# Moving one tile's gate chain, the x^T scaling and one weight load to other slots in a hybrid decoder layer

## The chip, the cores and the metric

The kernel runs on one core of a Trainium2 chip. The metric is device time in microseconds (us). The time before is the median of three runs, 1319.21 us (1318.01 to 1319.58).

## What is computed

The reference is a decoder layer with two kinds of token mixers that share one input and one output projection (batch 1, 2048 positions, width 1024, float32):

```python
xn = rms_norm(h, ln_g)
proj = jnp.einsum('bsd,de->bse', xn, w_in)
b_gate, c_gate, x_conv, g_conv, x_lru, g_lru = jnp.split(proj, splits, axis=-1)
y_conv = short_conv_mixer(b_gate, c_gate, x_conv, conv_w)
y_conv = headwise_rms_norm(y_conv, N_CONV_HEADS, conv_out_g) * jax.nn.silu(g_conv)
y_lru = rg_lru_mixer(x_lru, lru_conv_w, lru_conv_b, w_a, b_a, w_i, b_i, lam)
y_lru = headwise_rms_norm(y_lru, N_LRU_HEADS, lru_out_g) * jax.nn.silu(g_lru)
h = h + jnp.einsum('bse,ed->bsd', jnp.concatenate([y_conv, y_lru], axis=-1), w_out)
...
# rg_lru_mixer, on u = causal_depthwise_conv(x_lru, width 4) + bias:
r, i = sigmoid(gate maps of u per head)
a = exp(8 * r * log_sigmoid(lam))
h_t = a_t * h_{t-1} + sqrt(1 - a_t^2) * (i_t * u_t)      # along the positions
```

The layer's final `rms_norm` follows. All sums are in float32.

## The kernel before

**Numbers.** Every float32 matrix operand is cut into a high part (a cast by ScalarE to fp32r) and a low part (value minus high part, by VectorE). One block product is three matmuls: high by high, high by low, low by high (`mm`, L1009). In names of tiles, `s` is a weight operand (high and low side by side), `th` and `tl` are the high and low parts of the x^T operand, `raw` a raw weight piece of 256 KB, `traw` a raw piece of x^T.

**Steps and slots.** The input projection is made in 24 steps for each half of the positions (1024 each), named "l" (recurrent tile: x_lru and its gate g_lru), "a" and "b" (convolution: c_gate and x_conv, then b_gate and g_conv). Each step makes four 128x512 result blocks called 11, 12, 21 and 22 and hands each to a `put` function. The first four steps of the first half (`plain`, `products`) use plain products, since the operand set isn't complete yet; from step 4 on a seven-product scheme is used, with operands `T[0..6, j]` of x^T (j = 0..3) and `Sn[n][0..6]` of the weights. Before each of these products `tick()` is called: that is one slot, with 12 matmuls. `at(k, f)` puts `f` off to the k-th slot from now. All instructions are given out in the order in which this Python program runs them; each engine, and SyncE's queue of transfers (SP), takes its own in that order. So a slot number is a place in every engine's queue, not a time.

**The first tile.** `lru0 = lru(0, 0)` (L696) is the recurrent step 0. Its blocks 11 and 21 are made from unnormalised x^T and multiplied by the row norms later (`RAW`, then `lru0(11, None, rsb[0])`). After block 12 has come, `put` lists the rest of the tile by slot: `c0`, `cj` (the width-4 convolution, u), `sth`/`stl` (the cut of u), `gates(0)`, `gates(1)` (small matmuls on TensorE, L740), `sigs` (sigmoids), `s0` to `s5` (products, tanh, exp, sqrt, and `s5` the scan over positions), `out_` (`finish`: gain and gate, store, square, sums by head). `u` is a tile with one buffer: the next recurrent tile's `c0` writes the buffer that this tile's `s5` and, before, its output use.

**The other work of that stage.** `squares` and `rs0` make the row norms, `roots` turns them into a row (`rsb[0]`), `second(j)` makes the second block of x^T, `scaled(j)` multiplies the raw x^T by the norms and casts it, `scaled_lo(j)` makes its low part, `bit(j)` makes the sums of x^T blocks that operands 1, 2 and 6 need. `s_hi`, `s_lo` cut raw weights for the plain steps. `after1`, `after2`, `after3` hand these out among the slots of the steps 1, 2 and 3: slots 1 to 4, 5 to 12 and 13 to 20. Slot 21 is the first of step 4.

**Step 4 and on.** In a step the first product goes to a bank that ScalarE copies away (`q1`, L1435) before the second product of the same bank may start; between the two lies a slot with the seventh product of the step before, which step 4 does not have.

**The second half.** Operands of the weights are read back from `sd` in device memory (`s<-sd`, `s_loads`, L238) except for three steps (`redone`: 27, 28 and 29), whose raw weights are loaded anew into four of eight `raw` pieces (`load_s`, L326) and cut again. At the half's start (steps 24 and 25) the same pieces hold raw x^T (`traw`) until `Change.sixth` (L472) has used them in the last slot of step 25. `load_next(n + 2)` in slot s = 3 of a step gives the load out.

Of the kernel before, what the change touches and what calls it, by code (L numbers as in the profile page):

```python
# [14 lines left out]
AF = mybir.ActivationFunctionType  # L15
ALU = mybir.AluOpType

P = 128
D = 1024
S = 2048  # L20
C = 512
NC = S // C
NB = C // P
# [15 lines left out]
def hymba_kernel(ctx: ExitStack, tc: tile.TileContext, x, xt, w_in, par, lamc, w_gate, w_out, final_g, out):  # L39
# [103 lines left out]
    def at(slots, *fs):  # L143
        if slots == 0:
            for f in fs:
                f()
        else:
            due.append([slots, fs])
# [12 lines left out]
    def tt(out, a, b, op, eng=None):  # L161
        (eng or nc.vector).tensor_tensor(out=out, in0=a, in1=b, op=op)  # L162
# [483 lines left out]
            summed[0] = 0  # L646
            at(0 if h else 7, lambda: head_norms(h))

    def finish(d0, h, kt, y, sil, gain, to=None):
        z = sil if to is None else to  # L650

        def f1():
            nc.vector.scalar_tensor_tensor(out=z, in0=y, scalar=gain, in1=sil,
                                           op0=ALU.mult, op1=ALU.mult)

        def store():
            for i in range(2):
                nc.sync.dma_start(yd[2 * h + i][:, :, kt, :].rearrange("b p t -> p b t"),
                                  z[:, i * C:(i + 1) * C].rearrange("p (b t) -> p b t", b=NB))

        at(d0, f1)
        at(d0 + (1 if kt == KT and h == 0 else 2), store)
        at(d0 + 2, lambda: nc.scalar.activation(out=y, in_=y, func=AF.Square))
        at(d0 + 3, lambda: head_sums(h, kt, y))

    def silu(g, late=0, eng=None):
        sg = [None]

        def f1():
            sg[0] = wt("ig", "sg", bufs=IG)  # L670
            nc.scalar.activation(out=sg[0], in_=g, func=AF.Sigmoid)  # L671

        at(2 + late, f1)
        at(4 + late, lambda: tt(g, g, sg[0], ALU.mult, eng or nc.gpsimd))

# [15 lines left out]
    LO, HI = slice(0, 64), slice(64, P)  # L693
    N2 = 2 * C

    def lru(h, k, late=0, early=0):  # L696
        o1 = wt("o1", "xl", n=N2 + 4)
        g = wt("o2", "gl", bufs=O2)
        if h == 0:
# [32 lines left out]
        def gates(i):  # L732
            sl = slice(i * C, (i + 1) * C)
            if i == 0:
                v["r"], v["i"] = wt("r", "r"), wt("ig", "i", bufs=IG)
            v["ps"] = ps = []
            for j in range(2):
                ps.append(pss.tile([P, C], F32, tag="s", name="gate"))
                for n in range(2):
                    nc.tensor.matmul(ps[j], v["gw"][n][:, j, :], v["st"][j][:, sl],  # L740
                                     start=(n == 0), stop=(n == 1))

        def sigs(i):
            sl = slice(i * C, (i + 1) * C)
            for j, (hi, lo) in enumerate(((LO, HI), (HI, LO))):
                for g_, src, bias in ((v["r"], hi, BA), (v["i"], lo, BI)):
                    nc.scalar.activation(out=g_[hi, sl], in_=v["ps"][j][src], func=AF.Sigmoid,  # L747
                                         bias=pt[src, bias + k:bias + k + 1])
# [28 lines left out]
                nc.vector.tensor_copy(hl[:, k:k + 1], r[:, N2 - 1:N2])  # L777

        def out_():
            finish(0, h, KT + k, v["r"], g, pt[:, LG + k:LG + k + 1], v["u"] if h == 0 and k == 0 else None)  # L780

        def gw():
            v["gw"] = load_gate_w(k)
# [1 line left out]
        def put(which, bank, other):  # L785
            dst = {11: o1[:, 4:4 + C], 12: o1[:, 4 + C:4 + N2], 21: g[:, 0:C], 22: g[:, C:N2]}[which]
            combine(dst, bank, other)
            if other is RAW:
                return
            if which == 12:  # L790
                at(1, c0)
                at(2, lambda: cj(1), lambda: cj(2), keep, gw)
                at(3, lambda: cj(3))
                for slots, *fs in ((5 - early, sth), (6 - early, stl), (8, lambda: gates(0)), (8, lambda: sigs(0)),
                                   (10, lambda: gates(1)), (11 - h - early, lambda: sigs(1)), (12, s1, s0),
                                   (13, s1b), (14, s2, s3), (15, s4), (16, s5), (17, out_)):
                    at(slots + late, *fs)
            if which == 21:
                silu(g, late, nc.vector if late or not h else None)

        return put

# [253 lines left out]
    with tc.manual_schedule(engines={ENG.PE, ENG.Activation, ENG.DVE, ENG.Pool, ENG.SP}):  # L1056
# [44 lines left out]
        def s_lo(m, i, eng=None):  # L1101
            low(Wr[m][i], Sp[m][i], eng)
# [54 lines left out]
                products(0, raw[0], part, j, (0, 4), j == 0)  # L1157
        for b in range(NB, 2 * NB):
            norm_rows(b)
        lru0 = lru(0, 0)  # L1160
        lru0(11, raw[0][0], RAW)
        lru0(21, raw[0][1], RAW)

# [2 lines left out]
        def squares(b, eng=None):  # L1166
            for n in range(2):
                v, acc = xh[b][n], (rs0, rest)[n][:, b:b + 1]
                if eng is None:
                    nc.scalar.activation(out=v, in_=v, func=AF.Square, accum_out=acc)  # L1170
                else:
                    eng.scalar_tensor_tensor(out=v, in0=v, scalar=1.0, in1=v, op0=ALU.mult, op1=ALU.mult,
                                             accum_out=acc)

        squares(0)
        squares(1)
        squares(2, nc.vector)

        def second(j):
            for n, tag in ((1, "tl6"), (3, "th6")):  # L1180
                tr[j][n] = tp_.tile([P, C], F32, tag=f"{tag}{j}", name="traw")
            for i in range(2):
                turn(1, j + i * NB, tr[j][2 * i + 1], i)
            B12 = T[3, j] = t_tile(3, j)
            nc.scalar.copy(B12[0], tr[j][1])
            Tp[j].hi(5)
            low(tr[j][1], B12)
            Tp[j].lo(5)
# [4 lines left out]
                    second(j - 2)  # L1193
                products(1, raw[1], part, j, (0, 4))

        squares(3)
        tt(rs0, rs0, rest, ALU.add)
        nc.scalar.activation(out=rs0, in_=rs0, func=AF.Sqrt, scale=1.0 / D, bias=eps)
        nc.vector.reciprocal(out=rs0, in_=rs0)
        conv0 = conv_a(0, 0)  # L1200
        conv0(21, raw[1][1], RAW)

# [7 lines left out]
        def scaled(j):  # L1210
            for i in (0, 4):
                v = tr[j][i // 2]
                nc.vector.scalar_tensor_tensor(out=v, in0=v, scalar=gain(j + i), in1=rsb[0],  # L1213
                                               op0=ALU.mult, op1=ALU.mult)
                Tp[j].hi(i)

        def scaled_lo(j):
            for i in (0, 4):
                Tp[j].lo(i)
# [3 lines left out]
            nc.sync.dma_start(sd[0][i], S0[i].bitcast(F32))  # L1223
        c12, c22 = bank(), bank()
        for j in range(NB):
            if j + 2 < NB:
                second(j + 2)
            for cc, n in ((c12, 0), (c22, 2)):
                mm(cc, Sp[0], T, n, j, j == 0, False, k=3)
                mm(cc, Sp[0], T, n + 1, j, False, j == NB - 1, k=5)  # L1230
                if j == 1 and n == 0:
                    roots()
                    lru0(11, None, rsb[0])
                    lru0(21, None, rsb[0])
            if j >= 1:
                scaled(j - 1)
        scaled(3)
        lru0(22, c22, None)
        lru0(12, c12, None)
        second_half()  # L1240
# [40 lines left out]
                yield which, cc[which]  # L1281

        def after1(s):
            if s < 2:
                for i in (2 - 2 * s, 3 - 2 * s):
                    s_hi(2, i)
                for i in (2 - 2 * s, 3 - 2 * s):
                    s_lo(2, i)
            if s % 2 == 0:
                scaled_lo(s // 2)  # L1290
            do_bits(2)
            if s == 2:
                conv0(11, raw[1][0], rsb[0])
                conv0(22, kept[22], None)
# [6 lines left out]
        Wr.append(load_s(3))  # L1301

        def after2(s):
            if s in (0, 4):
                scaled_lo(2 + s // 4)
            if s % 2 == 0:
                s_hi(3, (2, 3, 0, 1)[s // 2])
            do_bits(1)
            if s % 2 == 0:
                s_lo(3, (2, 3, 0, 1)[s // 2])  # L1310
            if s > 5:
                for j in (2 * s - 12, 2 * s - 11):
                    T[6, j] = t_tile(6, j)
                    nc.scalar.copy(T[6, j][0], t6[j])

        put = conv_b(0, 0)
        for which, b in plain(2, (22, 12, 11, 21), after2):
# [3 lines left out]
        def after3(s):  # L1321
            if s in (1, 2, 3, 4, 6, 7):
                prep(4, (0, 1, 2, 3, 0, 4, 5)[s - 1])
            if s >= 6:
                js = (2 * s - 12, 2 * s - 11)
                for j in js:
                    T[3, j] = t_tile(3, j)
                    nc.scalar.copy(T[3, j][0], tr[j][1])
                for j in js:
                    low(tr[j][1], T[3, j])  # L1330
                at(s - 5, lambda: [low(t6[j], T[6, j]) for j in js])

        put = lru(0, 1)
        for which, b in plain(3, (11, 12, 22, 21), after3):
            if which == 12:
                kept[0] = b
            else:
                put(which, b, None)
# [4 lines left out]
        for n in range(PLAIN, N):  # L1343
# [31 lines left out]
            for s in range(6 if late else 8 if new or last else 7):  # L1375
# [33 lines left out]
                elif s > 0:  # L1409
                    if i == 2 and not late and held[0] is None or i == 1 and late:  # L1410
                        held[0] = []
                    if i != 2 or kind != "o" or not late:
                        prep(n + 1, s - 1)
                if s == 3:
                    load_next(n + 2, 3 if late else 4)
                if i == 6 and not late and s < 4:
                    if pend is not None:
# [90 lines left out]
```

## Time and profile before

| | us |
|---|---|
| median of 3 runs (lowest, highest) | 1319.21 (1318.01, 1319.58) |
| profiled execution, its own time | 1316.47 |
| its span, first to last instruction | 1314.5 |
| TensorE (PE) busy | 1285.9 (98%) |
| VectorE (DVE) busy | 1034.5 (79%) |
| ScalarE (ACT) busy | 753.8 (57%) |
| GpSimd (POOL) busy | 157.0 (12%) |
| granted TensorE clock, mean over the span | 0.993 |

The profiled execution took 2.0 us more than its span, and 2.7 us (0.2%) less than the median. "PE" is a matmul, "PEld" a weight load, "SPq" a transfer being issued by SyncE. In the timeline a row has start, length, engine, line, operation, output and inputs, shape, count, and in brackets the idle time of the engine before it and what ended it. `L162` is the helper `tt` for every elementwise VectorE operation on two tiles, so tiles tell more than lines there.

### The profile page before, as it was taken

The page shows a single profiled execution, that of the slowest core. Times are in us where ns is not written, and L with a number is a line of the kernel's source. Part 1 is how long each engine was busy: PE and PEld are TensorE (multiplying, and loading weights), DVE is VectorE, ACT ScalarE, POOL GpSimd, SP SyncE. Part 2 cuts the span into 40 slices and gives each one's busy share as a digit, 9 for nine tenths or more (in the row PEclk, how much of TensorE's full clock was granted, in tenths as well). Part 3 has the DMA queues.
Part 4 walks back from the last instruction along what each step waited for, and adds up shares of the span by engine and source line. Part 5 has one row for each costly group of instructions (what it writes and reads, how often), then busy time and mean ns, then how long its engine had stood idle before and what let it go on. Part 6 is the DMA issues. An engine that isn't in the chain of part 4 may idle for free.

```text
span 1314.5 us, 16625 instructions
## 1 busy us (share of the span) xinstructions
PE 1285.9 (98%) x5666; PEld 1060.5 (81%) x5666; DVE 1034.5 (79%) x1343; ACT 753.8 (57%) x1152; POOL 157.0 (12%) x143
## 2 busy tenths in 40 slices
PE   9979999999999999899999999999999999999997
PEld 8758888888888888677888888888888888888886
DVE  6788897999999998968566676667549877659886
ACT  8676867676675767665554545364457433445443
POOL 0000000233323320001010110102011000000000
PEclk9989999999999999999999999999999999999999
DMA  9206887898999888521889999999779897698754
GB/s 349 73 16 229 296 306 259 297 349 285 339 308 327 297 295 296 168 89 45 261 305 296 335 354 331 343 342 376 239 268 325 269 272 249 214 403 298 243 178 160
DMA packets 158244, 351.08 MB, mean 267 GB/s; under 512 B 16976, under 2 KB 51792, under 8 KB 158160
## 3 DMA queue, kind: packets, MB, share of 16 engines
q1 hardware_dynamic: 153552, 333.97, 73.5%
q0 software_dynamic: 4320, 15.73, 3.1%
q8 instruction: 45, 0.74, 0.2%
q14 instruction: 39, 0.32, 0.1%
q10 hardware_dynamic: 288, 0.32, 0.1%
HBM read 216.59 MB, written 133.37 MB: 266 GB/s over the span
## 4 chain that ended last, share of the span: by engine, by line
PE 82%; DVE 9%; DMA 4%; ACT 2%; issue 2%; SPq 0%; POOL 0%; DVEq 0%; ACTq 0%; POOLq 0%
PE bank L1014 78%; PE gate L740 2%; DVE tl L162 2%; PE bank L1151 2%; DMA tl<-td 1%; DMA s<-so 1%; DVE s L162 1%; DVE traw L162 1%; DMA raw<-yd 1%; DVE ob L162 1%; DVE u L712 0%; PE spin L541 0%; DVE traw L1213 0%; DMA s<-sd 0%; DVE st L162 0%
## 5 line engine op out<-in xcount | busy, mean ns | idle before, releaser
L1014 PE MATMUL bank<-th,s 128*128 128x512 f32 x3568 | 1109.4, 390 | 9.0 <-DMA s<-sd 5.6
L1014 PEld LDWEIGHTS bank<-th,s 128*128 128x128 f32 x3568 | 671.3, 188 | 151.6 <-DMA s<-sd 6.1
L1014 PE MATMUL bank<-tl,s 128*128 128x512 f32 x1784 | 695.4, 390 | 1.7 <-DVE tl L162 1.7
L1014 PEld LDWEIGHTS bank<-tl,s 128*128 128x128 f32 x1784 | 335.7, 188 | 72.0 <-DVE tl L162 2.1
L162 DVE TENSOR_TENSOR s<-raw,s 128x512 fp32r<-128x512 f32 (+1 forms) x151 | 104.0, 710 | 25.0 <-ACT s L212 20.5
L212 ACT CAST s<-raw 128x512 fp32r<-128x512 f32 x140 | 84.7, 618 | 42.8 <-PE bank L1014 29.2
L162 POOL TENSOR_TENSOR s<-raw,s 128x512 fp32r<-128x512 f32 x39 | 72.7, 1875 | 198.4 <-ACT s L212 141.1
L162 DVE TENSOR_TENSOR tl<-traw,th 128x512 fp32r<-128x512 f32 x92 | 61.5, 709 | 21.1 <-ACT th L450 10.7
L162 DVE TENSOR_TENSOR s<-s,s 128x512 fp32r<-128x512 f32 x105 | 74.3, 708 | 0.0
L212 ACT CAST s<-s 128x512 fp32r<-128x512 f32 x105 | 65.0, 619 | 10.2 <-DVE s L162 10.1
L712 DVE SCALAR_TENSOR_TENSOR u<-xl,pt,u 128x1024 f32<-128x1024 f32 x48 | 61.8, 1288 | 7.9 <-ACT u L708 7.4
L1435 ACT COPY q<-bank 128x512 f32<-128x512 f32 x57 | 33.4, 585 | 49.7 <-PE bank L1014 47.1
L162 POOL TENSOR_TENSOR gb<-gb,sg 128x1024 f32<-128x1024 f32 x8 | 20.1, 2509 | 308.3 <-ACT sg L671 308.3
L831 DVE SCALAR_TENSOR_TENSOR t<-p,pt,t 128x1024 f32<-128x1024 f32 x32 | 44.7, 1396 | 13.2 <-ACT t L828 12.6
L747 ACT ACTIVATE r<-gate,pt 64x512 f32<-64x512 f32 x64 | 43.8, 684 | 18.0 <-PE gate L740 17.2
L162 DVE TENSOR_TENSOR st<-u,st 64x512 fp32r<-64x512 f32 x64 | 49.3, 771 | 2.0
L162 DVE TENSOR_TENSOR raw<-raw,zr 128x512 f32<-128x512 f32 x64 | 41.1, 684 | 8.1 <-DMA zr<-rsd 7.7
L1439 ACT COPY rr<-bank 128x512 f32<-128x512 f32 x30 | 17.6, 586 | 50.3 <-PE bank L1014 50.3
L747 ACT ACTIVATE i<-gate,pt 64x512 f32<-64x512 f32 x64 | 43.8, 685 | 1.1
L1445 ACT COPY u<-bank 128x512 f32<-128x512 f32 x30 | 17.5, 585 | 46.4 <-PE bank L1014 46.3
L1439 ACT COPY u<-bank 128x512 f32<-128x512 f32 x27 | 15.8, 585 | 48.6 <-PE bank L1014 48.6
L162 DVE TENSOR_TENSOR traw<-traw 128x512 f32<-128x512 f32 x60 | 42.2, 707 | 1.6 <-DMA traw<-in_w_out_dram 0.6
(206 smaller groups left out, 1316.1 us busy)
## 6 DMA issues: line engine op xcount, KB each, us to landing
sd<-s SPq DMA_DIRECT2D x144, 512.0 KB
s<-sd SPq DMA_DIRECT2D x144, 512.0 KB
raw<-in_w_in_dram SPq DMA_DIRECT2D x108, 256.0 KB
raw<-yd SPq DMA_DIRECT2D x64, 256.0 KB
traw<-in_w_out_dram SPq DMA_DIRECT2D x64, 256.0 KB
so<-so SPq DMA_DIRECT2D x22, 512.0 KB
s<-so SPq DMA_DIRECT2D x22, 512.0 KB
yd<-gb SPq DMA_DIRECT2D x32, 256.0 KB
```

The lines of the kernel that those rows point to most:

```text
L162: (eng or nc.vector).tensor_tensor(out=out, in0=a, in1=b, op=op)
L212: nc.scalar.copy(dst[i][0], val(i))
L712: nc.vector.scalar_tensor_tensor(out=v["u"], in0=o1[:, 1 + j:1 + j + N2], scalar=lw[j], in1=v["u"], op0=ALU.mult, op1=ALU.add)
L740: nc.tensor.matmul(ps[j], v["gw"][n][:, j, :], v["st"][j][:, sl], start=(n == 0), stop=(n == 1))
L747: nc.scalar.activation(out=g_[hi, sl], in_=v["ps"][j][src], func=AF.Sigmoid, bias=pt[src, bias + k:bias + k + 1])
L831: nc.vector.scalar_tensor_tensor(out=tcur["t"], in0=p[:, 2 + j:2 + j + N2], scalar=cw[j], in1=tcur["t"], op0=ALU.mult, op1=ALU.add)
L1014: nc.tensor.matmul(bank, a[:, js], b, start=start and n == 0, stop=stop and n == 2, skip_group_check=more)
L1151: nc.tensor.matmul(bk, s[w][:, j * P:(j + 1) * P], t[v], start=first, stop=last, skip_group_check=True)
L1435: nc.scalar.copy(q1, bk["A"])
L1439: nc.scalar.copy(u2, bk["A"])
L1445: nc.scalar.copy(rr, bk["A"])
```

## The change

- `lru0` is made with `late` 5, `early` 1 and the new argument `wait` 1: its `sth` goes from slot 5 to 9, `stl` from 6 to 10, `gates(0)` from 8 to 14, `gates(1)` from 10 to 16, `s0` and the tanh from 12 to 17, the rest by 5 slots (the scan `s5` from 16 to 21, `out_` from 17 to 22). Its gate's silu goes from slots 2 and 4 to 7 and 9 and writes a tile of its own (`gs`), into which the output is then written too; the output no longer goes into `u`.
- `squares(3)` goes from ScalarE to VectorE, and the norms' root goes ahead of `second(0)`; `roots` goes from the second to the first block of the loop.
- The eight products of `scaled` go ahead to the second block (j = 1), the eight casts and the eight low parts to the third and fourth (j = 2, 3).
- The weight cuts of step 2 all go to slot 1; those of step 3 keep their slots but in the order 0, 1, 2, 3.
- The casts and low parts of operands 3 and 6 go to one j in each of slots 17 to 20; step 3 makes its blocks in the order 12, 22, 11, 21.
- In step 25 the load of the raw weights of step 27 is put off by three slots.

```diff
-    def finish(d0, h, kt, y, sil, gain, to=None):
-        z = sil if to is None else to
+    def finish(d0, h, kt, y, sil, gain):
...
-            nc.vector.scalar_tensor_tensor(out=z, in0=y, scalar=gain, in1=sil,
+            nc.vector.scalar_tensor_tensor(out=sil, in0=y, scalar=gain, in1=sil,
...
-    def silu(g, late=0, eng=None):
+    def silu(g, late=0, eng=None, into=None):
...
-        at(4 + late, lambda: tt(g, g, sg[0], ALU.mult, eng or nc.gpsimd))
+        at(4 + late, lambda: tt(g if into is None else into(), g, sg[0], ALU.mult, eng or nc.gpsimd))
...
-    def lru(h, k, late=0, early=0):
+    def lru(h, k, late=0, early=0, wait=0):
...
-            finish(0, h, KT + k, v["r"], g, pt[:, LG + k:LG + k + 1], v["u"] if h == 0 and k == 0 else None)
+            finish(0, h, KT + k, v["r"], v.get("g", g), pt[:, LG + k:LG + k + 1])
...
-                for slots, *fs in ((5 - early, sth), (6 - early, stl), (8, lambda: gates(0)), (8, lambda: sigs(0)),
-                                   (10, lambda: gates(1)), (11 - h - early, lambda: sigs(1)), (12, s1, s0),
+                for slots, *fs in ((5 - early, sth), (6 - early, stl), (8 + wait, lambda: gates(0)), (8 + wait, lambda: sigs(0)),
+                                   (10 + wait, lambda: gates(1)), (11 - h - early + wait, lambda: sigs(1)), (12, s1, s0),
                                    (13, s1b), (14, s2, s3), (15, s4), (16, s5), (17, out_)):
                     at(slots + late, *fs)
             if which == 21:
-                silu(g, late, nc.vector if late or not h else None)
+                into = (lambda: v.setdefault("g", wt("hl", "gs", bufs=HL))) if h == 0 and k == 0 else None
+                silu(g, late, nc.vector if late or not h else None, into)
...
-        lru0 = lru(0, 0)
+        lru0 = lru(0, 0, 5, 1, 1)
...
         squares(2, nc.vector)
+        squares(3, nc.vector)
+        tt(rs0, rs0, rest, ALU.add)
+        nc.scalar.activation(out=rs0, in_=rs0, func=AF.Sqrt, scale=1.0 / D, bias=eps)
+        nc.vector.reciprocal(out=rs0, in_=rs0)
...
-        squares(3)
-        tt(rs0, rs0, rest, ALU.add)
-        nc.scalar.activation(out=rs0, in_=rs0, func=AF.Sqrt, scale=1.0 / D, bias=eps)
-        nc.vector.reciprocal(out=rs0, in_=rs0)
...
+
+        def scaled_hi(j):
+            for i in (0, 4):
                 Tp[j].hi(i)
...
         for j in range(NB):
+            if j == 1:
+                scaled(0)
+                scaled(1)
             if j + 2 < NB:
                 second(j + 2)
+            if j == 1:
+                scaled(2)
+                scaled(3)
+                lru0(11, None, rsb[0])
+                lru0(21, None, rsb[0])
+            if j >= 2:
+                for n in (2 * j - 4, 2 * j - 3):
+                    scaled_hi(n)
+                    scaled_lo(n)
             for cc, n in ((c12, 0), (c22, 2)):
...
-                if j == 1 and n == 0:
+                if j == 0 and n == 0:
                     roots()
-                    lru0(11, None, rsb[0])
-                    lru0(21, None, rsb[0])
-            if j >= 1:
-                scaled(j - 1)
-        scaled(3)
...
         def after1(s):
-            if s < 2:
-                for i in (2 - 2 * s, 3 - 2 * s):
+            if s == 0:
+                for i in (2, 3, 0, 1):
                     s_hi(2, i)
-                for i in (2 - 2 * s, 3 - 2 * s):
+                for i in (2, 3, 0, 1):
                     s_lo(2, i)
-            if s % 2 == 0:
-                scaled_lo(s // 2)
...
         def after2(s):
-            if s in (0, 4):
-                scaled_lo(2 + s // 4)
             if s % 2 == 0:
-                s_hi(3, (2, 3, 0, 1)[s // 2])
+                s_hi(3, s // 2)
+                s_lo(3, s // 2)
             do_bits(1)
-            if s % 2 == 0:
-                s_lo(3, (2, 3, 0, 1)[s // 2])
-            if s > 5:
-                for j in (2 * s - 12, 2 * s - 11):
-                    T[6, j] = t_tile(6, j)
-                    nc.scalar.copy(T[6, j][0], t6[j])
...
-            if s >= 6:
-                js = (2 * s - 12, 2 * s - 11)
-                for j in js:
-                    T[3, j] = t_tile(3, j)
-                    nc.scalar.copy(T[3, j][0], tr[j][1])
-                for j in js:
-                    low(tr[j][1], T[3, j])
-                at(s - 5, lambda: [low(t6[j], T[6, j]) for j in js])
+            if s >= 4:
+                j = s - 4
+                for i, v in ((3, tr[j][1]), (6, t6[j])):
+                    T[i, j] = t_tile(i, j)
+                    nc.scalar.copy(T[i, j][0], v)
+                for i, v in ((3, tr[j][1]), (6, t6[j])):
+                    low(v, T[i, j])
...
-        for which, b in plain(3, (11, 12, 22, 21), after3):
+        for which, b in plain(3, (12, 22, 11, 21), after3):
...
-                if s == 3:
+                if s == 3 and late and n + 2 in redone:
+                    at(3, lambda n=n: load_next(n + 2))
+                elif s == 3:
                     load_next(n + 2, 3 if late else 4)
```

More of the change, by code (lines that the diff above doesn't have):

```diff
@@ L658, in store @@
                 nc.sync.dma_start(yd[2 * h + i][:, :, kt, :].rearrange("b p t -> p b t"),
-                                  z[:, i * C:(i + 1) * C].rearrange("p (b t) -> p b t", b=NB))
+                                  sil[:, i * C:(i + 1) * C].rearrange("p (b t) -> p b t", b=NB))
         at(d0, f1)
```

## The prediction

> **What bounds the kernel now.** The page comes first: which engine is full over the span.
>
> ```profile
> span 1314.5 us, 16625 instructions
> PE 1285.9 (98%) x5666; PEld 1060.5 (81%) x5666; DVE 1034.5 (79%) x1343; ACT 753.8 (57%) x1152; POOL 157.0 (12%) x143
> ```
>
> TensorE is busy all but 28.6 us, and the change takes no matmul away. So it can only earn idle time of TensorE and what the clock loses after it. Second view: whom TensorE waited for (total us, times, longest). Third: its timeline at those waits, and the chain, which gives a slot of 12 matmuls (228 in 51.69 us, so 2.72 us) and four gate matmuls (0.93).
>
> ```profile
> PE gate L740 <- DVE st L162: 9.4, 1, 9.4
> PE bank L1014 <- DMA s<-sd: 5.6, 1, 5.6
> PE bank L1014 <- ACT q L1435: 2.6, 3, 1.1
> PE bank L1014 <- DVE tl L162: 1.7, 1, 1.7
> ...
> 72.97 0.76 PE L740 MATMUL gate<-st,bh 128*128 128x512 f32 x1 [9.43 <-DVE st L162]
> 73.53 0.63 PE L740 MATMUL gate<-st,bl 128*128 128x512 f32 x1
> 76.88 0.63 PE L1014 MATMUL bank<-th,s 128*128 128x512 f32 x2
> 82.59 0.50 PE L1014 MATMUL bank<-tl,s 128*128 128x512 f32 x1 [1.68 <-DVE tl L162]
> 117.59 0.50 PE L1014 MATMUL bank<-th,s 128*128 128x512 f32 x1 [0.68 <-ACT q L1435]
> ...
> 556.86 0.80 PE L1014 MATMUL bank<-th,s 128*128 128x512 f32 x1 [5.63 <-DMA s<-sd]
> 561.62 0.63 PE L1014 MATMUL bank<-th,s 128*128 128x512 f32 x2
> ...
> 138.05 0.93 PE gate L740 x4
> 138.98 51.69 PE bank L1014 x228
> ```
>
> The change touches four of these: the 9.43 at the first tile's gates (slot 8), 1.68 (slot 10, low parts of x^T), 0.68 (slot 23, second product of step 4) and 5.63 (step 26). After the long ones matmuls start 0.43 us apart instead of 0.227: 9 of them up to 76.88, 11 up to 561.62. That is 1.8 and 2.2 us more; after 0.68 there is nearly none. Fourth view, stretches:
>
> ```profile
> 44.00:63.50 19.50, 19.50 (x87) 15.84 (x85) 15.52 (x23) 10.99 (x18) 2.32 (x3) 1.00 0.19 54
> 63.50:85.00 21.50, 10.39 (x37) 8.08 (x37) 21.21 (x32) 11.96 (x20) 0.76 (x2) 0.76 0.08 25
> 85.00:117.60 32.60, 31.92 (x142) 26.10 (x140) 23.67 (x31) 25.73 (x37) 0.00 (x0) 1.00 0.33 105
> 117.60:131.50 13.90, 13.90 (x61) 11.52 (x62) 13.77 (x17) 8.12 (x13) 1.74 (x3) 1.00 0.79 295
> ```
>
> The third busy figure is VectorE's: while TensorE stands (63.5 to 85) it works 21.21 of 21.5 us, so the first stage hangs on VectorE's queue. From 85 on ScalarE (the fourth) is the fuller one, 25.73 us of 32.6.
>
> **The change, part by part.** Durations of the stage, all before:
>
> ```profile
> 49.32 1.29 DVE L162 TENSOR_TENSOR s<-raw,s 128x512 fp32r<-128x512 f32 x2 [3.46 <-ACT s L1097]
> 53.06 2.60 DVE L712 SCALAR_TENSOR_TENSOR u<-xl,pt,u 128x1024 f32<-128x1024 f32 x2
> 72.14 2.82 DVE L162 TENSOR_TENSOR st<-u,st 64x512 fp32r<-64x512 f32 x4
> 102.50 2.29 DVE L774 TENSOR_TENSOR_SCAN r<-r,u 128x1024 f32<-128x1024 f32 x1
> ...
> 93.08 1.28 ACT L759 ACT_TABLE_LOAD   x1
> 109.28 1.07 ACT L663 ACTIVATE r<-r 128x1024 f32<-128x1024 f32 x1
> 110.74 1.15 ACT L1328 CAST th<-traw 128x512 fp32r<-128x512 f32 x2
> 114.78 0.59 ACT L807 COPY xl<-bank 128x512 f32<-128x512 f32 x1
> 115.45 1.25 ACT L708 ACTIVATE u<-xl,pt 128x1024 f32<-128x1024 f32 x1
> 116.95 0.59 ACT L1435 COPY q<-bank 128x512 f32<-128x512 f32 x1 [0.25 <-PE bank L1014]
> ...
> L747 ACT ACTIVATE r<-gate,pt 64x512 f32<-64x512 f32 x64 | 43.8, 684 | 18.0 <-PE gate L740 17.2
> ```
>
> Records overlap by about 0.1 us, so queued work is counted from start to start: small VectorE operations 0.60 (1.29 - 0.69), wide ones 1.13 to 1.25, ScalarE casts 0.52, bank copies 0.48, 1024-wide functions 1.0, gate sigmoids 0.70.
>
> *The norms sooner.* Two squares go from ScalarE to VectorE (1.3 us there); ScalarE waits some 1.6 us for them before the root, then no longer has its own two. The second x^T blocks are up to 0.9 us later. Cover: whether TensorE loses that doesn't matter, because it waits later anyway (below).
>
> *The x^T scaling.* The row of norms is there at 36.5 instead of 38.9 us. Eight products, two low parts and two multiplications (7.7 us) end at 44.6; the eight low parts then run where VectorE stood idle 3.46 us before 49.32. The 1.68 wait goes: they are ready some 17 us before slot 9.
>
> *Gates in slot 14.* TensorE starts slot 1 seven slots before its old wait (63.54), at 44.5; without waits slot 14 comes at 44.5 + 13 x 2.72 = 79.9. VectorE's list from 44.6 on to the cut of u: eight low parts, weight lows, x^T sums, convolutions. Up to the fourth x^T set's third sum these are 43 small ones (26.0), three wide products of u (3.7), two of the convolution (2.5), the gate's product (1.1) and four halves of `st` (2.8), 36.1 us, and 2.8 us in which weight lows stand behind their casts (ScalarE does the convolution's 1.06 us product first). 3.8 us of it come after the first pair of `st`, which is ready at 44.6 + 32.3 + 2.8 = 79.7. The gates come just in time; what they are late, the next wait loses less. So the 9.43 and its 1.8 us go.
>
> *What is late next: slot 23.* The moved chain now meets the head of step 4. In slot 21 the first tile's scan and the next tile's `c0` come together; `c0` writes the buffer of `u` that the scan reads, so ScalarE waits for the scan, and behind `c0` in ScalarE's queue stands the copy `q1`, for which TensorE must wait before the second product (slot 22 has no matmuls). Before, the scan was 13 us older (102.50) and `c0` (115.45) waited for no scan.
>
> ScalarE: that third sum leaves VectorE at 44.6 + 36.1 + 2.8 = 83.5, a cast and a bank copy follow, and from 84.6 it has no gap: 8 sigmoids of the gates (5.6), 13 casts (6.8), 4 bank copies (1.9), six 1024-wide functions (6.1), two table loads (2.6): 23.0, so 107.6. VectorE: the square root stands in that list at 102.5, the third cast pair of operands 3 and 6 ends at 104.0; then two low parts (1.2), one wide product (1.1), four low parts (2.4), the scan (2.3): 110.9. Then `c0` 1.06 and `q1` 0.48 with handovers: the second product starts at 112.5, where before it started at 117.59. TensorE wants it at 44.5 + 21 x 2.72 + 2 x 0.93 = 103.5, so a new wait of about 9 us stands where 0.68 stood. It costs the slow clock again; from the two long waits 1.8 and 2.2 I take 2.0. Net gain of the first stage: 5.1 - 2.0 = 3.1 us, of 14.1 that lie there. Bounds: 14.1 if nothing queues there; 0 if the queue is 3 us longer than listed. I take 3.1, since each row in the list is a duration of this stage.
>
> By the Trainium skill ("TensorE: Matmul & The Clock Gate", Part 1) an idle window of about 3.4 us halves the clock and a busy one of 3.4 us frees it; by that the loss is an estimated 1.7 us and the stage's gain 3.4. The rows (half rate over 3.9 and 4.8 us, nothing after 0.68) agree in kind and are a little longer.
>
> Behind slot 23: the tile's output product and sums (1.2 + 1.2 us) come after the scan, where before they were done. VectorE still reaches the next `st` at about 125 to 127, and slot 28 starts at 112.5 + 2.0 + 5 x 2.72 = 128.1 (before 131.3). So no further wait, with 1 to 3 us to spare. The order of step 3, the copies of operands 3 and 6, the own `gs` tile: same instructions, hidden by TensorE's wait; nothing. The number of table loads stays.
>
> *The raw load of step 27.* SP's queue, its waits, and who had time:
>
> ```profile
> 549.31 2.14 SPq L326 DMA_DIRECT2D raw<-in_w_in_dram  x4
> 551.54 3.03 SPq L238 DMA_DIRECT2D s<-sd  x5
> SPq L326 <- DVE traw L162: 12.9, 4, 12.2
> 548.56 2.49 DVE L162 TENSOR_TENSOR traw<-traw 128x512 f32<-128x512 f32 x4
> 551.54 5.28 DMA s<-sd
> 556.12 0.68 DVE L162 TENSOR_TENSOR s<-raw 128x512 f32<-128x512 f32 x1
> 562.75 0.69 DVE L162 TENSOR_TENSOR s<-raw,s 128x512 fp32r<-128x512 f32 x1 [5.22 <-ACT s L212]
> 568.52 0.69 DVE L162 TENSOR_TENSOR xx<-bank,rr 128x512 f32<-128x512 f32 x1 [4.47 <-PE bank L1014]
> 572.29 0.69 DVE L162 TENSOR_TENSOR gb<-bank,rr 128x512 f32<-128x512 f32 x1 [1.74 <-ACT rr L1445]
> ```
>
> SP stood 12.2 us at the first of the four raw loads, until VectorE (548.56) let the pieces go; the five operand loads of step 26 stood behind it, and the second (operand 3) ended TensorE's 5.63. Three slots later in the program the raw loads come behind operands 3 and 2, which then wait only for a buffer that TensorE frees: step 26's second slot would start at 551.1, so operand 5 of step 25 was done near 539.3, and operand 3 lands by 539.4 + 5.3 = 544.7, 6 us early. The raw loads still wait for 548.56, so they issue when they did. Operands 4 and 5 stay behind them, land near 557 to 559 and are wanted at about 563. Gain 5.63 + 2.2 of clock + rounding = 8.1: the slot after next started at 565.5 and now starts at 557.4. VectorE can follow: it stood idle 11.4 us here. From 572.29 its chain is dense, but it begins with TensorE's product and shifts whole. Bounds: 0 to 8.1; I take 8.1.
>
> Sum: 3.1 + 8.1 = 11.2 us off the profiled execution's 1316.47 (span 1314.5): 1305.3; the median of the runs stood 2.7 above it: 1319.2 - 11.2 = 1308.0.
>
> **The rivals.**
>
> *A, no new wait at slot 23.* If `c0` and `q1` come in time, the whole 14.1 is earned: 1319.2 - 14.1 - 8.1 = 1297.0. For it: only ScalarE's and VectorE's order stand against it. Against: 23.0 us of ScalarE work stand in a stretch of 20 us, so even without the scan `q1` ends at 109.2 (net 6 to 7 us, 1304.5).
>
> The Trainium skill ("TensorE: Matmul & The Clock Gate", Architectural detail) says that ScalarE and VectorE take their queues strictly in order, which speaks against A. The trace shows such a queue later, where a multiplication waited 3.00 us and the next in VectorE's queue ran only behind it:
>
> ```profile
> 598.87 0.69 DVE L162 TENSOR_TENSOR gl<-bank,u 128x512 f32<-128x512 f32 x1 [3.00 <-DMA yd<-gl]
> ```
>
> *B, step 26 keeps its wait.* If operand 3 waits for something else than the raw loads, only 3.1 is earned: 1316.1. Against: SP's 12.2.
>
> *C, slower.* Raw set 27 lands too late for the first sums of step 27, which VectorE met without a wait at 556.1; behind them stand its products for TensorE. Read by the letter, three slots are 8.2 us: the sums at 564 still lie in the 11.4 us of idle time, less the 8.1 by which all moves up; a cost of about 5. It costs 1 us per us from 559.4 on, and the kernel becomes slower by more than 0.2% only beyond 559.4 + 11.2 + 2.6 = 573: say 1323 at 574.5. Against: 1 MB went out in 2.14 us of issue and was there within 7 us.
>
> *D, no effect:* the gates are late again at slot 14 by as much as they were at 8 (9 us more VectorE work than listed), and B: within 0.2%.
>
> **How the numbers follow.** Likeliest case 0.65: 1308.0, by itself 1304 to 1311.5. A 0.13 (1297 to 1304), B 0.13 (1313 to 1317, half of it within 0.2%), D 0.05, C 0.04. A measurement of this kernel can tell about 0.2% (2.6 us) from no change. Faster by over 0.2%: 0.65 + 0.13 + 0.06 = 0.84; within 0.2%: 0.07 + 0.05 = 0.12; slower: 0.04. The range, 1300.5 to 1313.5, holds the likeliest case, most of A and the edge of B.
>
> **What would show it.** Right: no wait of the gates on `st` over 1 us before 90; a wait of TensorE for ACT `q` of 7 to 10 us ending near 112.5, the scan ending just before `c0`; half clock after it; no wait on `s<-sd` in step 26, raw loads after two operand loads there. Wrong: `q` wait under 4 us (A), `s<-sd` still there (B), VectorE waiting for `raw` in step 26 (C).

## The result, and the profile after

| | before | after |
|---|---|---|
| median, us (lowest, highest) | 1319.39 (1318.01, 1320.23) | 1307.05 (1305.73, 1308.55) |
| profiled execution, its own time / span | 1316.47 / 1314.5 | 1305.73 / 1303.8 |
| mean granted TensorE clock | 0.993 | 0.995 |

Both medians are of four executions (the 1319.21 above is of three). The ratio is 0.9908, 95% interval 0.9891 to 0.9925: the change makes the kernel 12.3 us faster by the medians and 10.7 us by the two profiled executions. The profiled execution lies 2.9 us below its median in before and 1.3 in after, so the medians show 1.6 us more than the profiles.

The page of after, and the waits of TensorE in its span (total us, times, longest):

```profile
span 1303.8 us, 16629 instructions
PE 1283.6 (98%) x5666; PEld 1060.6 (81%) x5666; DVE 1035.4 (79%) x1347; ACT 751.3 (58%) x1148; POOL 156.0 (12%) x143
```
```profile
PE bank L1013 <- ACT q L1436: 10.5, 3, 8.6
PE spin L541 <- POOL xl L698: 1.6, 1, 1.6
PE bank L1013 <- DVE ob L162: 0.7, 1, 0.7
PE bank L1013 <- ACT rr L1446: 0.6, 1, 0.6
```

The waits for `st`, for `tl` and for `s<-sd` are gone (9.4, 1.7 and 5.6 us before); one of 8.6 us for `q` has come. It stands in step 4, between the first and the second product. TensorE's timeline of after there, with the gates of the first tile (80.31), those of step 5 (128.41) and those of the tile in step 25 of the second half (547.10):

```profile
80.31 0.39 PE L738 MATMUL gate<-st,bh 128*128 128x512 f32 x1
...
112.86 0.80 PE L1013 MATMUL bank<-th,s 128*128 128x512 f32 x1 [8.63 <-ACT q L1436]
113.46 0.63 PE L1013 MATMUL bank<-tl,s 128*128 128x512 f32 x1
113.89 1.05 PE L1013 MATMUL bank<-th,s 128*128 128x512 f32 x2
...
117.05 0.40 PE L1013 MATMUL bank<-tl,s 128*128 128x512 f32 x1
...
128.41 0.39 PE L738 MATMUL gate<-st,bh 128*128 128x512 f32 x1
...
547.10 0.39 PE L738 MATMUL gate<-st,bh 128*128 128x512 f32 x1
```

The gates have no bracket: they waited for nothing. After the 8.63 us, ten matmuls take 117.05 - 112.86 = 4.19 us where ten at 0.227 take 2.27: 1.9 us lost. Why `q` is late stands in the two queues, VectorE's (cut of u, scan, next cut) and ScalarE's (first gate sigmoid, last bank copy, `c0`, `q1`):

```profile
77.90 2.84 DVE L162 TENSOR_TENSOR st<-u,st 64x512 fp32r<-64x512 f32 x4
...
108.70 2.28 DVE L772 TENSOR_TENSOR_SCAN r<-r,u 128x1024 f32<-128x1024 f32 x1
...
125.20 2.84 DVE L162 TENSOR_TENSOR st<-u,st 64x512 fp32r<-64x512 f32 x4
...
84.31 0.69 ACT L745 ACTIVATE r<-gate,pt 64x512 f32<-64x512 f32 x1
...
106.94 0.58 ACT L806 COPY xl<-bank 128x512 f32<-128x512 f32 x1
111.10 1.24 ACT L706 ACTIVATE u<-xl,pt 128x1024 f32<-128x1024 f32 x1 [3.58 <-DVE r L772]
112.25 0.56 ACT L1436 COPY q<-bank 128x512 f32<-128x512 f32 x1
```

`c0` (111.10) waits 3.58 us for the scan, and the copy `q` runs behind it. From the first sigmoid to the bank copy at 106.94 ScalarE's list has no gap.

The second half: SyncE's issues around step 26, then VectorE:

```profile
531.59 7.86 SPq L238 DMA_DIRECT2D s<-sd  x5
546.26 2.14 SPq L326 DMA_DIRECT2D raw<-in_w_in_dram  x4
548.49 1.33 SPq L238 DMA_DIRECT2D s<-sd  x3
...
553.09 0.68 DVE L162 TENSOR_TENSOR s<-raw 128x512 f32<-128x512 f32 x1
...
561.17 0.69 DVE L162 TENSOR_TENSOR gb<-bank,rr 128x512 f32<-128x512 f32 x1 [1.74 <-ACT rr L1446]
```

Five operand transfers now go out ahead of the raw loads of step 27 (546.26), two of which stood behind these before; VectorE's first sum of that raw set (553.09) has no wait. The last of these rows stood at 572.29 before: 11.12 us sooner, 3.05 of which were there already at the gates of step 25 (550.15 before, 547.10 now). So the first stage earned 3.05 us and the load 8.07. Of the 11.12, some 0.45 is given back near 1182 us, where a wait for `ob` takes 0.66 us instead of 0.20.

### The profile page after: what moved, and what is told of

It reads as the page before. It is cut to its first block, busy times and chain, and to the rows that moved or that the text cites. A ratio compares the mean times of both kernels' runs of the same rounds, so it can differ in the third digit from the quotient of the medians.

```text
span 1303.8 us, 16629 instructions
## 1 busy us (share of the span) xinstructions
PE 1283.6 (98%) x5666; PEld 1060.6 (81%) x5666; DVE 1035.4 (79%) x1347; ACT 751.3 (58%) x1148; POOL 156.0 (12%) x143
## 4 chain that ended last, share of the span: by engine, by line
PE 83%; DVE 6%; DMA 3%; ACT 3%; issue 1%; SPq 0%; DVEq 0%; ACTq 0%
PE bank L1013 81%; PE gate L738 2%; DMA tl<-td 2%; DVE s L162 1%; DVE tl L162 1%; DVE traw L162 1%; DMA raw<-yd 1%; DVE ob L162 0%; DMA zr<-rsd 0%; DVE u L710 0%; DVE r L772 0%; ACT s L1096 0%; ACT sg L669 0%; DMA yd<-gl 0%; DVE u L162 0%
## 5 line engine op out<-in xcount | busy, mean ns | idle before, releaser
L1013 PE MATMUL bank<-th,s 128*128 128x512 f32 x3568 | 1108.1, 390 | 11.8 <-ACT q L1436 10.5
L162 DVE TENSOR_TENSOR tl<-traw,th 128x512 fp32r<-128x512 f32 x92 | 61.5, 709 | 21.5 <-ACT th L450 10.7
```

Of the source, the lines that this page charges most:

```text
L1013: nc.tensor.matmul(bank, a[:, js], b, start=start and n == 0, stop=stop and n == 2, skip_group_check=more)
```

## The experiments

**The load alone.** This is the kernel before with only one edit:

```diff
-                if s == 3:
+                if s == 3 and late and n + 2 in redone:
+                    at(3, lambda n=n: load_next(n + 2))
+                elif s == 3:
                     load_next(n + 2, 3 if late else 4)
```

> The kernel before with only the raw load of step 27 put off by three slots. Theory (the two halves of the change are independent, and this one removes the wait for the operand loads of step 26): no wait of TensorE on s<-sd, the 9.43 and 1.68 of the first stage as before; 8.1 us less than before, 1311.3. Rival (the operand loads were late for another reason): the 5.6 us wait stays, 1319.

Measured: 1310.04 us (1309.08 to 1310.29), ratio 0.9935 (0.9923 to 0.9947) to 1318.71 of before: 8.7 us. The waits of its TensorE:

```profile
PE gate L740 <- DVE st L162: 9.7, 2, 9.4
PE bank L1014 <- ACT q L1437: 2.6, 3, 1.1
...
PE bank L1014 <- DVE tl L162: 0.9, 1, 0.9
```

No `s<-sd` is left, and the waits of the first stage stand nearly as before (`tl` 0.9 instead of 1.7 us). The load alone earns its 8 us, and VectorE's first sum of the raw set that is issued later (556.41) has no wait.

**All but the load.** This is the kernel after without that edit.

> The changed kernel with the raw load of step 27 back in its old slot. Theory: the wait on s<-sd of 5.6 us and 2.2 us of slow clock come back, the first stage as in the changed kernel (wait for the q copy of 8.6 us near 113): 8.1 us more than the changed kernel, 1315.2. Rival (the load matters only together with the rest): 1307.

Measured: 1315.88 us (1314.37 to 1317.64), ratio 0.998 (0.9971 to 0.9989): 2.8 us. The `q` wait of after and the `s<-sd` wait of before stand in one kernel:

```profile
PE bank L1013 <- ACT q L1434: 10.5, 3, 8.7
PE bank L1013 <- DMA s<-sd: 6.6, 1, 6.6
```

8.7 and 2.8 us make 11.5, against 12.3 for both: the two parts add up, within the scatter of these runs (about 1 us).

**The shift without the sooner scaling.** This is after with `squares(3)`, the norms' root, `roots`, `scaled`, the low parts of x^T and the weight cuts of step 2 where before has them. The gates in slots 14 and 16, all else that the change moves, and the load are as in after. Three of the places, with cuts between them:

```diff
-        squares(3, nc.vector)
...
+        squares(3)
...
+            if j >= 1:
+                scaled(j - 1)
...
+            if s % 2 == 0:
+                scaled_lo(s // 2)
```

> The changed kernel with the norms, roots, x^T scaling and the weight cuts of step 2 in their old places; the gates stay in slot 14. Theory (VectorE's list is the limit, moving the gates only moves the wait): no wait at the gates, but some 11 us at slot 10 for the low parts of x^T near 80, then some 7 us at slot 23, which starts near 122 instead of 113; 1317 to 1319. Rival (the moved gates earn the first stage): the low parts wait 2 us or less, 1307 to 1310.

Measured: 1319.42 us (1316.87 to 1320.75), ratio 1.0006 (0.9997 to 1.0015), just above the range that was expected. Its waits:

```profile
PE bank L1013 <- DVE tl L162: 11.8, 2, 11.0
PE bank L1013 <- ACT q L1430: 9.4, 3, 7.5
```

The load, which this kernel has too, gives 1310.04 by itself; the shift, with what goes along with it (`gs`, the copies of operands 3 and 6, the order of step 3), therefore costs 9.4 us: TensorE no longer waits at slot 8 for `st`, runs on to slot 10 and waits there 11.0 us for the low parts of x^T, which stand in the same VectorE queue, and then 7.5 us at slot 23 as well, which starts at 124.93, 3 us later than was expected.

**The scaling without the shift.** This is the kernel of the first experiment with the sooner norms, `roots`, scaling and weight cuts of step 2 of after. The gates are in slots 8 and 10, the scan in 16; the output into `u`, the copies of operands 3 and 6 and the order of step 3 are as before. One line of its difference to after:

```diff
-        lru0 = lru(0, 0, 5, 1, 1)
+        lru0 = lru(0, 0)
```

> The changed kernel without the moved gates: norms, scaling, weight cuts and the late load as in the change; the first tile's gates in slot 8 and all that follows as before (output again into u, order of step 3 as before). Theory (the sum of waits is set by VectorE's and ScalarE's work up to slot 23, and the moved chain only puts the scan behind the copies of step 4): a wait of about 6 us at the gates near 70, none at slot 10, under 1 us at slot 23, which starts near 111 to 113; 1304.5 to 1306.5, so 1 to 2 us less than the changed kernel. Rival (moving the gates is worth what its row says): 6 to 8 us more than the changed kernel, 1313 to 1315.

Measured: 1304.83 us (1303.66 to 1305.26), ratio 0.9896 (0.9883 to 0.991). Its TensorE and VectorE:

```profile
69.39 0.77 PE L740 MATMUL gate<-st,bh 128*128 128x512 f32 x1 [6.08 <-DVE st L162]
...
112.27 0.50 PE L1014 MATMUL bank<-th,s 128*128 128x512 f32 x1 [0.68 <-ACT q L1443]
...
126.00 0.39 PE L740 MATMUL gate<-st,bh 128*128 128x512 f32 x1
...
97.19 2.29 DVE L774 TENSOR_TENSOR_SCAN r<-r,u 128x1024 f32<-128x1024 f32 x1
```

The gates wait 6.08 us, the scan is over long before `c0`, and slot 23 costs what it did before. The gates of step 5 start 2.4 us sooner than in after (126.00 against 128.41). The four kernels with the load, side by side:

| medians, us | gates in slot 8 | in slot 14 |
|---|---|---|
| scaling as before | 1310.04 | 1319.42 |
| scaling sooner | 1304.83 | 1307.05 |

The columns differ in the copies of operands 3 and 6 and the order of step 3 too, so "shift" stands for all of these. The sooner scaling carries the first stage's gain; the shift by six slots costs 2.2 us beside it (2.4 in the traces; the intervals of the two ratios to before overlap, and 1307.05 stands against a before of 1319.39, the others against 1318.71) and 9.4 without it.

**`c0` behind the copy.** This is after with one line changed:

```diff
-                at(1, c0)
+                at(2 if h == 0 and k == 1 else 1, c0)
```

> The kernel after, with one edit: the first convolution product (c0) of the second recurrent tile is put one slot later, so that in ScalarE's queue the copy q1 stands ahead of c0 instead of behind it. Theory (two things set slot 23: c0 waits for the scan, and ScalarE's own list, which ends at 107 without the scan): TensorE's wait for q falls from 8.6 to about 4 us, its end from 112.9 to about 108; but the next tile's chain then comes later by as much as c0 does, and waits of up to 1 us appear at the sixth slot of step 4 and at the next gates near 125, so the gates of step 5 start 1.5 to 2.8 us sooner than in the kernel after: 1304.3 to 1305.6. Rival 1 (the scan alone was the cost): the wait is gone, 8.6 and some 2 us of clock are earned, 1296.5. Rival 2 (the wait is for a bank or an operand, not for the queue): nothing changes, 1307.

Measured: 1305.21 us (1305.05 to 1305.34), ratio 0.9899 (0.9885 to 0.9912): 1.8 us less than after, or 0.9 when each is taken from the before that was run beside it (the intervals of the two ratios overlap). In the traces the gates of step 5 start 2.1 us sooner. ScalarE, then TensorE:

```profile
107.68 0.60 ACT L1436 COPY q<-bank 128x512 f32<-128x512 f32 x1
111.37 1.25 ACT L706 ACTIVATE u<-xl,pt 128x1024 f32<-128x1024 f32 x1 [0.21 <-DVE r L772]
...
108.33 0.80 PE L1013 MATMUL bank<-th,s 128*128 128x512 f32 x1 [3.86 <-ACT q L1436]
...
126.29 0.47 PE L738 MATMUL gate<-st,bh 128*128 128x512 f32 x1 [1.67 <-DVE st L162]
```

`q` now runs ahead of `c0`, and the wait falls by 4.8 us, to what ScalarE's list alone makes of it. But `c0` still waits for the scan, the next tile's `st` is no sooner, and 1.67 us of it come back at the gates of step 5, 0.53 at a copy before. The wait for the scan is the larger part of the 8.63, and not all that stands there.

**Two tanh more.** This is after with the first tile's tanh run three times:

```diff
-            nc.scalar.activation(out=v["T"], in_=v["r"], func=AF.Tanh, scale=nklam[:, k:k + 1])
+            for _ in range(3 if h == 0 and k == 0 else 1):
+                nc.scalar.activation(out=v["T"], in_=v["r"], func=AF.Tanh, scale=nklam[:, k:k + 1])
```

> The kernel after, with the first recurrent tile's 1024-wide hyperbolic tangent run three times instead of once (the same result): two more instructions of 1.0 us in ScalarE's list ahead of the scan. Theory (the gapless list of ScalarE from the gates on, then VectorE's up to the scan, sets when slot 23 may start): the wait for q grows from 8.6 to about 10.6 us and all behind it shifts: 1309.1, between 1308.5 and 1309.5. Rival (VectorE's own list sets the scan, ScalarE has room): under 0.5 us more, 1307.0 to 1307.5.

Measured: a median of 1308.55 us (1308.24 to 1309.71 in four executions; a fifth took 6787 us and is left out). Ratio 0.9926 (0.9912 to 0.9939). ScalarE, VectorE and TensorE:

```profile
92.69 3.53 ACT L755 ACTIVATE T<-r,nklam 128x1024 f32<-128x1024 f32 x3
...
111.34 2.29 DVE L773 TENSOR_TENSOR_SCAN r<-r,u 128x1024 f32<-128x1024 f32 x1
...
115.50 0.79 PE L1014 MATMUL bank<-th,s 128*128 128x512 f32 x1 [11.00 <-ACT q L1437]
...
130.67 0.39 PE L738 MATMUL gate<-st,bh 128*128 128x512 f32 x1
```

One tanh took 1.15 us in after, so 2.38 us were added; the wait grew from 8.63 to 11.00, by 2.37, and the gates of step 5 came 2.26 us later. (The medians differ by 1.5 us, or by 2.4 when each is taken from the before that was run beside it; the scatter of after's is about 1.5.) ScalarE's list ahead of the scan sets slot 23 one to one.

**Filling the wait.** This is after with matmuls that nothing reads, in the slot of step 4 that has none:

```diff
+                    elif n == 4:
+                        fill = pss.tile([P, C], F32, tag="s", name="fill")
+                        for _ in range(36):
+                            nc.tensor.matmul(fill, T[0, 0][0][:, 0:P], T[0, 0][0], start=True, stop=True)
                     continue
```

> The kernel after, with 36 matmuls of 128x512 that nothing reads put into slot 22 of step 4, where TensorE otherwise issues nothing and then waits 8.63 us for q. 36 at 0.227 us are 8.2 us, so TensorE works nearly up to the end of that wait and the second product still starts near 112.9. Theory (after the wait 10 matmuls start 0.43 us apart because TensorE stood, a loss of 1.9 us): the matmuls behind 112.9 start 0.227 us apart at once, the wait shrinks to under 1 us, and the gates of step 5 start 1.5 to 1.9 us sooner, since VectorE's next st (125.2, first pair at 126.6) just allows it: 1305.3. Rival 1 (the half rate comes from something else at that place, such as operands or the new bank): 10 slow matmuls stay, 1307.0. Rival 2 (the fillers themselves are slow or start late): 1308 to 1311.

Measured: 1305.55 us (1305.3 to 1307.22), ratio 0.9903 (0.9887 to 0.992). TensorE:

```profile
104.88 8.32 PE L1430 MATMUL fill<-th 128*128 128x512 f32 x36
113.69 0.50 PE L1013 MATMUL bank<-th,s 128*128 128x512 f32 x1 [0.49 <-ACT q L1440]
114.03 0.39 PE L1013 MATMUL bank<-tl,s 128*128 128x512 f32 x1
114.26 0.62 PE L1013 MATMUL bank<-th,s 128*128 128x512 f32 x2
...
127.43 0.39 PE L738 MATMUL gate<-st,bh 128*128 128x512 f32 x1
```

The product behind the wait runs at full rate from its first matmul (this execution was 0.8 us late before the wait, and comes to the next gates 1.0 us sooner than after: 1.8 us). So the slow matmuls come from TensorE having stood, not from their place.

**The gates two slots later instead of six.** In the kernel without the shift `st` is ready near 69.4 us, and slot 10 comes at 69. (In after `st` starts only at 77.90, since its cut stands in slots 9 and 10.) So this is after with the gates in slots 10 and 12, and `sth`, `stl`, the scan and the output back in 5, 6, 16 and 17:

```diff
+                if h == 0 and k == 0:
+                    for slots, *fs in ((5, sth), (6, stl), (10, lambda: gates(0)), (10, lambda: sigs(0)),
+                                       (12, lambda: gates(1)), (12, lambda: sigs(1)), (13, s1, s0),
+                                       (13, s1b), (14, s2, s3), (15, s4), (16, s5), (17, out_)):
+                        at(slots, *fs)
+                    return
```

> The kernel after, with the first recurrent tile's gates in slots 10 and 12 instead of 14 and 16 and what follows them in slots 13 to 17 instead of 17 to 22 (the sooner norms and scaling and the later load are kept). Theory: st is ready at about 69.5 to 70 wherever the gates stand, as in the kernel without the shift; slot 10 comes at 69, so the gates wait under 1 us; the second gates may wait 1 to 3 us for the small banks; the scan ends by about 102, so q1 comes in time and slot 23 waits 1 to 2 us at 105 to 108. The gates of step 5 start at 122 to 124 (128.4 in the kernel after): 1301, between 1299.5 and 1302.5. Rival (VectorE's dense list up to the next st bounds that place at 125, whatever the first tile does): as without the shift, 1304.8.

Measured: 1301.68 us (1301.29 to 1301.88), ratio 0.9872 (0.9857 to 0.9887), the fastest of all: 16.8 us less than before, 5.4 less than after, or 4.5 when each is taken from the before that was run beside it (the intervals of the two ratios to before do not overlap). TensorE, then VectorE's scan and next cut:

```profile
69.32 0.40 PE L738 MATMUL gate<-st,bh 128*128 128x512 f32 x1
...
78.18 0.50 PE L738 MATMUL gate<-st,bh 128*128 128x512 f32 x1 [2.05 <-ACT i L745]
79.58 0.79 PE L738 MATMUL gate<-st,bh 128*128 128x512 f32 x1 [0.66 <-ACT i L745]
...
109.52 0.50 PE L1019 MATMUL bank<-th,s 128*128 128x512 f32 x1 [0.68 <-ACT q L1442]
...
123.68 0.47 PE L738 MATMUL gate<-st,bh 128*128 128x512 f32 x1 [0.27 <-DVE st L162]
...
95.44 2.28 DVE L772 TENSOR_TENSOR_SCAN r<-r,u 128x1024 f32<-128x1024 f32 x1
...
122.85 2.84 DVE L162 TENSOR_TENSOR st<-u,st 64x512 fp32r<-64x512 f32 x4
```

The scan is 13 us sooner than in after, and `q` costs 0.68. What stands instead are 2.05 and 0.66 us at the second gates, for the banks of the first, which ScalarE's sigmoids free late, and 1.4 us of slow matmuls behind them. The rival of this run said that VectorE's list bounds the next `st` at 125; it starts at 122.85, so that bound was not there. Whether VectorE is the next one was not tried.

## Why the prediction was right

The mechanism and the sizes came out as worked out, step by step:

- *Gates in slot 14.* The first pair of `st` was predicted at 79.7, TensorE at the slot at 79.9. VectorE's four halves start at 77.90, so the first pair is done near 79.3; the gates start at 80.31 without a wait.
- *Slot 23.* ScalarE's gapless list was to start at 84.6 and end at 107.6; it starts at 84.31, and its last copy ends at 107.5. The scan was to end at 110.9; it ends at 110.98. The second product was to start at 112.5 after 9 us; it starts at 112.86 after 8.63. The clock's part was put at 2.0, between a 1.8 and a 2.2 that the rows give as 1.9 and 2.3; it is 1.9. Net gain of the stage 3.1 predicted, 3.05 measured.
- *Rival A.* It failed for the two reasons given: the scan (4.8 us of the wait go when `q` runs ahead of `c0`) and ScalarE's list (3.86 us stay even then; `q` ends at 108.3, where the prediction had 109.2 without the scan). The Trainium skill ("TensorE: Matmul & The Clock Gate", Architectural detail) has ScalarE and VectorE take their queues strictly in order; the trace agrees: `q`, whose bank was ready (its product ended near 104.2), ran only behind `c0`, at 112.25.
- *The load.* 8.1 predicted, 8.07 in the traces, 8.7 by medians of the kernel with the load alone. The raw set of step 27, issued at 546.26, made nobody wait; rivals B and C fell with that.
- *The sum.* 11.2 predicted, 11.12 at 561.17. The profiled executions differ by 10.74, since 0.45 goes at `ob`; the medians by 12.3. The forecast set the median 2.7 us above the profile, as in before, and in after it stands 1.3 above it. So most of what 1308.0 misses of 1307.05 is scatter of the runs, and not a term of the sum.

What the prediction did not ask is what each half of the first stage is worth. It let the shift remove "the 9.43 and its 1.8 us" and the scaling only 1.68. The runs show another split: the sooner scaling alone cuts the gates' wait from 9.43 to 6.08, because the eight low parts now run where VectorE stood idle for 3.47 us, so that the cut of u starts at 68.55 instead of 72.54, and earns 5.2 us (1310.04 to 1304.83); the shift then removes 6.08 and its slow clock and brings 8.63 and 1.9. Taken by itself the shift is a loss. The predicted sum is untouched by this, as both were in it.

## What to carry to other kernels

A wait on a busy engine's queue moves when the consumer is put later: the place where the chain next meets the critical engine has to be costed with the same list, and here 10.5 us (8.63 and 1.9) came for the 8.2 (6.08 and 2.1) that the moved gates saved beside the sooner scaling. The best slot of the three tried is the one where the operand is just ready (slot 10, at 69 us), not the latest that still has work to cover; everything behind in the chain moves along. Four transfers that waited 12.2 us for their buffers held up five behind them in SyncE's queue: issue first what is free to go, and look for the first row that stands in the queue, not for the one that TensorE waits for.

## What the runs showed of the hardware

The slow matmuls after a wait do not grow with the wait. Counted from the first matmul until the starts are 0.227 us apart again: 1.9 us lost after 8.63, 2.1 after the 6.08 of the kernel without the shift, 1.7 after the 3.86 of the kernel with `c0` later, 1.5 after the 10.98 of the kernel without the sooner scaling, 2.3 after the 5.63 of before. After 1.67 us (the gates of step 5 with `c0` later) the granted clock stays at 1.00. But 2.05 and 0.66 with 0.74 us of work between them cost 1.4.

The granted clock (third figure from the end) shows where the loss comes from. In after it falls to half at 106.5, in the middle of the wait, and is back at 116.75:

```profile
106.60:112.86 6.26, 0.00 (x0) 0.00 (x0) 6.12 (x8) 2.68 (x5) 0.00 (x0) 0.50 0.53 190
112.86:116.70 3.84, 3.83 (x9) 3.07 (x10) 3.77 (x5) 3.82 (x6) 0.00 (x0) 0.50 0.59 147
```

Read in steps of 0.1 us, it stays at half for 10.24 us here and at the first long wait of before (66.56 to 76.80), for 6.83 at the second (554.66 to 561.49) and for 3.41 in the kernel with `c0` later: three, two and one times 3.413. The two slow stretches of before (76.80 to 554.66) lie 140 times that apart. So in these runs the clock changes on a grid of 3.41 us that does not start with the wait, and the loss is half of what is left of the slow stretch when work begins: (116.75 - 112.86) / 2 = 1.9. The Trainium skill ("TensorE: Matmul & The Clock Gate", Part 1) puts the change down to a free-running window of about 3.4 us, so that the loss depends on where in the window work begins again; the trace agrees. That page halves the clock after an idle window; here a window that was idle in part was enough. In the kernel with the gates in slot 10 the clock fell at 79.0, 0.07 us into the second wait, after TensorE had stood for 2.1 of the last 3.41 us. The 1.68 us of before, within one such window, were not enough.
